# Context stores and input loads issued by GpSimd, and a count of 2.4 for the context's steps without weights

## The chip, the core and the metric

The kernel runs on one core of one Trainium2 chip. The core has five engines, each with its own instruction queue that is worked through in order: TensorE (PE, matrix products; PEld is its loading of weights), VectorE (DVE), ScalarE (ACT), GpSimd (POOL) and SyncE (SP, which here only issues transfers). Transfers between the device memory and the core's own memory (DMA) run on 16 DMA engines. The metric is the device time of one execution in microseconds (us).

## What is computed

Two transformer blocks run one after the other on 256 tokens of width 1024. The first block has a mixture of experts: 32 experts, four of them chosen for each token. The second block has two layers; it works on the latent tokens x and on a context of 256 further tokens. Cut to what matters:

```python
def moe_ffn(h, router_w, router_b, w_mlp1, b_mlp1, w_mlp2, b_mlp2):
    ...
    top_vals, top_idx = lax.top_k(logits, TOP_K)
    ...
    acc, _ = lax.scan(expert_step, acc0, (w_mlp1, b_mlp1, w_mlp2, b_mlp2, combine))

def second_block(x, c, ctx, c_ctx, ...):
    xc = ctx
    for l in range(DEPTH_2):
        ctx_out = l < DEPTH_2 - 1
        ...
        o, oc = token_mixers(modulate(x, sh1, sc1), modulate(xc, sh1c, sc1c), ...)
        x = layer_norm(DEEPNORM_ALPHA * x + g1 * (o @ w_out[l]), ...)
        x = layer_norm(DEEPNORM_ALPHA * x + g2 * swiglu(modulate(x, sh2, sc2), ...), ...)
        if ctx_out:
            xc = layer_norm(DEEPNORM_ALPHA * xc + g1c * (oc @ w_out[l]), ...)
            xc = layer_norm(DEEPNORM_ALPHA * xc + g2c * swiglu(modulate(xc, sh2c, sc2c), ...), ...)
    return x
```

The context xc does not depend on the first block. The latent tokens need from it, in each layer, only its keys and values and the final states of its linear attention.

## The kernel before

The program has three parts. In the first, the first block's attention runs and its router picks the experts. In the second, the 32 experts run, sorted by how many tokens they have: two of them with room for 128 tokens (rows), then sixteen with 64, then fourteen with 32. An expert's weights are twelve loads of 1 MB (`m_raw`), which SyncE issues into five buffers (`RAWS`); line 904 multiplies the first eight, line 962 the other four. Beside the experts the context of the second block runs. In the third part (`latent`) the latent tokens go through the second block's two layers.

The context is a generator (`context`, lines 1588 to 1667). Its steps yield a time, and `along` (line 1887) hands out credit: after each step of an expert the context gets 0.8, 1.45 or 3.2 (`SHARE`, for experts of 128, 64 and 32 rows) and advances until that is used up. Some steps work without weights: attention, the states of the linear attention (`gla_states`) and the linear attention itself (`gla`, with its decay steps in lines 1822 to 1826). These go through `dry`, which multiplies the time that they yield by `DRY`, so that they are spread further. After the last expert the rest of the context gets all the credit it wants.

This sets the order in which the code is written out. A scheduler then orders the instructions of each engine anew, by when it expects their inputs and the engine to be free. What runs is the order that it leaves on each engine.

The context's weights come by ScalarE's queue, in pieces of 512 KB (`w_raw`). Each is halved into two parts: ScalarE rounds it (`w_hi`, line 96) and GpSimd subtracts (`w_lo`, line 98). Each product is then three matmuls (lines 195 to 197). Four halved tiles fit. The products of the context go to the tile `c`, those of the latent part to `ps`.

The lines that the change touches: `keep` (line 1597) stores four tiles of keys and values (`nak`, `nav`, `gak`, `gav`) and later two states (`sf`, `sb`), once in each of two layers, so twelve stores; lines 1637 and 1642 load the context's input `x`, 1 MB, twice. The second load comes after the first layer's mixers, and `x` is scaled on GpSimd (line 1644, four instructions) before the output projection's sums are added to it. The small products of line 1543 (`ss`, on GpSimd, for a modulation) are placed in memory that other tiles have used before. The latent part reads the stored tiles back (line 1683), behind a branch (lines 1102 and 1103) that all engines pass after the last expert; more experts' work for overfull experts would stand behind it.

Of the kernel before, what the change touches and what calls it, by code (L numbers as in the profile page):

```python
# [37 lines left out]


SHARE = {128: 0.8, 64: 1.45, 32: 3.2}  # L40
DRY = 2.0
FILL = 0.8

FIRST = 2
# [87 lines left out]
class Build:  # L132
# [1455 lines left out]
    def context(self, w, ps, tag, saved):  # L1588


        nc, tc, io = self.nc, self.tc, self.io
        one = lambda n: tc.tile_pool(name=n, bufs=1, side="right")
        two = lambda n: tc.tile_pool(name=n, bufs=2, side="right")

        def keep(l, name, t):
            saved[l][name] = tc.dram_tile(list(t.shape), F32, name=f"kept_{name}_{l}")
            nc.sync.dma_start(saved[l][name], t)

        def halves(pu):
            return [pu.tile([P, KC, T], F32R, name=n) for n in ("uh", "ul")]  # L1600

        def mixers(l, u, pu, full):
            y = None
            with one("cg") as pg:
                o = {n: pg.tile(sh, F32, name=n) for n, sh in self.GLA_SHAPES + (self.FULL_SHAPES[2:] if full else ())}
                with one("cq") as pq:
                    o.update({n: pq.tile(sh, F32, name=n) for n, sh in self.SHAPES + (self.FULL_SHAPES[:2] if full else ())})
                    done = set()
                    with two("cp") as p2:
                        yield from self.projections(l, 1, u, o, w, p2, ps, tag, full, done)  # L1610
                    for n, _ in self.SHAPES:
                        keep(l, n, o[n])
                    if full:
                        y = halves(pu)
                        with two("ca") as p2:
                            yield from dry(self.attend(self.units(l, 1, o, None, done), *y, p2, ps, tag, done))
                with one("cl1") as p, two("cl2") as p2:
                    for n in ("sf", "sb"):
                        o[n] = p.tile([P, 64], F32, name=n)
                    yield from dry(self.gla_states(o, p2, ps, tag))  # L1620
                    for n in ("sf", "sb"):
                        keep(l, n, o[n])
                    if full:
                        yield from dry(self.gla(l, 1, o, None, *y, p, p2, ps, tag, done))
            return y

        def dry(steps):

            for c in steps:
                yield c and c * DRY  # L1630

        mod = [m[:, 1] for m in self.mod2]
        with one("cu") as pu:
            u = halves(pu)
            with one("cx") as px, two("ct") as p2:
                x = px.tile([P, KC, T], F32, name="x")
                nc.sync.dma_start(x, io["ctx"])
                yield from self.modulated(x, mod[0][:, 0:8], mod[0][:, 8:16], u, p2)
            y = yield from mixers(0, u, pu, True)
            with one("cx") as px:  # L1640
                x = px.tile([P, KC, T], F32, name="x")
                nc.sync.dma_start(x, io["ctx"])
                for k in range(0, KC, 2):
                    nc.gpsimd.tensor_scalar(x[:, k:k + 2], x[:, k:k + 2], ALPHA, None, op0=ALU.mult)
                for i in range(2):
                    with one("cf") as p:
                        acc = p.tile([P, KC, T], F32, name="acc")
                        if i == 0:
                            for ks in MIXED2:
                                yield from self.columns(acc, lambda k: (y[0][:, k], y[1][:, k]), ks, MIXED2[0][0], MIXED2[-1][1], w, ps, tag)  # L1650
                        else:
                            u = halves(pu)
                            with one("ch") as p1, two("ch2") as p2:
                                yield from self.modulated(x, *self.affine(mod[0], 1, 0, 0, p1), u, p2, None, normed)
                                self.settle(x, normed[0], 0, 0, p1)
                                yield from self.ffn(u, w, acc, p1, p2, ps, tag)
                        with two("cr2") as p2:
                            chunk, finish = self.norm(acc, mod[0][:, 24 * i + 16:24 * i + 24], x, px, p2, ps, tag)
                            for k in range(KC):
                                chunk(k)  # L1660
                                yield 0.4
                            normed = finish()
                            yield 1.8
                u = halves(pu)
                with two("ct") as p2:
                    yield from self.modulated(x, *self.affine(mod[1], 0, 0, 1, px), u, p2, None, normed)
                yield from mixers(1, u, pu, False)
# [410 lines left out]
```

## Time and profile before

| | us |
|---|---|
| median of 3 runs | 2369.41 |
| their range | 2366.2 to 2372.82 |
| profiled execution | 2358.65 |
| its span, first to last instruction | 2357.0 |

| engine | busy us | share of the span |
|---|---|---|
| TensorE matmuls | 2144.4 | 91% |
| TensorE loading weights | 1503.0 | 64% |
| VectorE | 1087.7 | 46% |
| ScalarE | 862.6 | 37% |
| GpSimd | 567.6 | 24% |

The execution moved 667.36 MB. The shares are means over parts with different limits, so that each part has to be read by itself. In the rows further down, a line of windows gives for each engine the busy time and, in brackets, the number of instructions; then the clock that TensorE was granted, as a share of full speed; the mean busy share of the 16 DMA engines; and what they moved. In a line of a timeline the brackets at the end tell how long the engine was idle before the instruction, and what ended the wait.

### The profile page before, as it was taken

Reading aid. Unit: us, or ns where it says so; the run is one execution under the profiler, and the core shown is the slowest. Engines: PE = TensorE matmul, PEld = TensorE weight load, DVE = VectorE, ACT = ScalarE, POOL = GpSimd, SP = SyncE. Lnnn points to the kernel's source line nnn. Section 1 sums busy time; section 2 is a strip of 40 time slices with the busy share of each in tenths; the row PEclk is TensorE's granted clock in tenths of the full one; section 3 lists DMA queues with packets and bytes.
Section 4 is the critical chain, followed back from the end, with each engine's and each line's share of the span. In section 5 each row is a group of like instructions: output and inputs, shape, how many; then the busy total and the mean of one; then the engine's idle time right before and its main releaser. Section 6 shows DMA issues by size and latency. Waiting matters only on the chain. (4 is left out here: it accounts for less than half of the span.)

```text
span 2357.0 us, 38285 instructions
## 1 busy us (share of the span) xinstructions
PE 2144.4 (91%) x15238; PEld 1503.0 (64%) x15239; DVE 1087.7 (46%) x2146; ACT 862.6 (37%) x1585; POOL 567.6 (24%) x335
## 2 busy tenths in 40 slices
PE   7899799999999988977999998968989999899998
PEld 4667533455444433524776765637879997788997
DVE  4765333221334322325443345227569767757434
ACT  2533201132232111213333333314555555466554
POOL 1001100122100000202444442504214443322442
PEclk8999799999999999977998999979999999999999
DMA  9867657899988899998999999993256754233553
GB/s 369 316 236 278 262 193 253 334 393 366 368 315 305 326 403 416 378 393 331 377 379 397 374 409 366 395 371 118 82 189 247 275 183 146 90 104 112 190 186 101
DMA packets 121721, 667.36 MB, mean 283 GB/s; under 512 B 14944, under 2 KB 16864, under 8 KB 62784
## 3 DMA queue, kind: packets, MB, share of 16 engines
q1 hardware_dynamic: 104016, 597.86, 67.5%
q10 hardware_dynamic: 17520, 66.99, 7.6%
q8 instruction: 122, 2.00, 0.3%
q14 instruction: 63, 0.52, 0.1%
HBM read 661.51 MB, written 3.28 MB: 282 GB/s over the span
## 5 line engine op out<-in xcount | busy, mean ns | idle before, releaser
L98 POOL TENSOR_TENSOR w_lo<-w_raw,w_hi 128x1024 fp32r<-128x1024 f32 x210 | 503.9, 2403 | 1098.8 <-ACT w_hi L96 890.1
L96 ACT ACTIVATE w_hi<-w_raw 128x1024 fp32r<-128x1024 f32 (+1 forms) x332 | 346.1, 1048 | 418.4 <-PE c L196 162.1
L904 PE MATMUL u<-m_raw,xT 128*64 128x512 f32 (+1 forms) x2048 | 396.0, 620 | 28.2 <-DMA m_raw<-in_w_mlp 28.2
L195 PE MATMUL ps<-uh,w_hi 128*128 128x256 f32 (+1 forms) x944 | 274.0, 291 | 10.4 <-ACT uh L1214 6.0
L197 PE MATMUL ps<-uh,w_lo 128*128 128x256 f32 (+1 forms) x944 | 270.5, 287 | 4.9 <-DVE w_lo L98 3.2
L196 PE MATMUL ps<-ul,w_hi 128*128 128x256 f32 (+1 forms) x944 | 270.7, 287 | 1.3 <-DVE ul L1215 1.2
L904 PEld LDWEIGHTS u<-m_raw,xT 128*64 128x64 f32 (+1 forms) x2048 | 103.8, 127 | 220.9 <-issue 172.5
L962 PE MATMUL y<-m_raw,aT 128*32 128x256 f32 (+1 forms) x1536 | 216.0, 507 | 19.1 <-DMA m_raw<-in_w_mlp 16.3
L98 DVE TENSOR_TENSOR w_lo<-w_raw,w_hi 128x1024 fp32r<-128x1024 f32 (+1 forms) x122 | 153.0, 1254 | 110.5 <-ACT w_hi L96 109.8
L195 PEld LDWEIGHTS ps<-uh,w_hi 128*128 128x128 f32 (+1 forms) x944 | 182.2, 193 | 17.7 <-ACT uh L1214 7.1
L197 PEld LDWEIGHTS ps<-uh,w_lo 128*128 128x128 f32 (+1 forms) x944 | 182.7, 194 | 5.9 <-DVE w_lo L98 3.9
L196 PEld LDWEIGHTS ps<-ul,w_hi 128*128 128x128 f32 (+1 forms) x944 | 183.0, 194 | 2.9 <-DVE ul L1215 2.0
L195 PE MATMUL c<-uh,w_hi 128*128 128x256 f32 (+1 forms) x584 | 172.0, 295 | 4.2 <-ACT uh L1214 3.1
L196 PE MATMUL c<-ul,w_hi 128*128 128x256 f32 (+1 forms) x584 | 170.7, 292 | 0.0
L197 PE MATMUL c<-uh,w_lo 128*128 128x256 f32 (+1 forms) x584 | 170.5, 293 | 0.0
L195 PE MATMUL ps<-hh,w_hi 128*128 128x256 f32 x560 | 163.8, 293 | 0.0
L197 PE MATMUL ps<-hh,w_lo 128*128 128x256 f32 x560 | 159.1, 284 | 1.2 <-DVE w_lo L98 1.2
L196 PE MATMUL ps<-hl,w_hi 128*128 128x256 f32 x560 | 159.4, 285 | 0.5 <-DVE hl L189 0.5
L962 PEld LDWEIGHTS y<-m_raw,aT 128*32 128x32 f32 (+1 forms) x1536 | 74.3, 129 | 131.8 <-issue 89.5
L914 DVE TENSOR_SCALAR glu<-u 128x512 f32<-128x512 f32 (+1 forms) x34 | 23.3, 687 | 236.4 <-PE u L904 236.3
L195 PEld LDWEIGHTS c<-uh,w_hi 128*128 128x128 f32 (+1 forms) x584 | 112.8, 193 | 25.1 <-issue 15.7
L196 PEld LDWEIGHTS c<-ul,w_hi 128*128 128x128 f32 (+1 forms) x584 | 113.2, 194 | 13.6 <-issue 10.9
(554 smaller groups left out, 3921.4 us busy)
## 6 DMA issues: line engine op xcount, KB each, us to landing
m_raw<-in_w_mlp SPq DMA_DIRECT2D x384, 1024.0 KB, 8.0
f_raw<-in_w_ada SPq DMA_DIRECT2D x47, 1024.0 KB, 7.1
w_raw<-in_w_ffn_in SPq DMA_DIRECT2D x88, 512.0 KB, 4.2
w_raw<-in_w_in SPq DMA_DIRECT2D x64, 512.0 KB, 5.0
w_raw<-in_w_ffn_in ACTq DMA_DIRECT2D x44, 512.0 KB, 8.6
w_raw<-in_w_ffn_out SPq DMA_DIRECT2D x44, 512.0 KB, 4.2
w_raw<-in_w_in ACTq DMA_DIRECT2D x34, 512.0 KB, 7.9
g_raw<-in_w_ada SPq DMA_DIRECT2D x16, 1024.0 KB, 8.4
```

Source lines behind the costliest of these rows:

```text
L96: nc.scalar.activation(hi, r, AF.Copy)
L98: e.tensor_tensor(lo, r, hi.bitcast(F32), op=ALU.subtract)
L195: nc.tensor.matmul(out, lh, rh, start=start, stop=False)
L196: nc.tensor.matmul(out, lh, rl, start=False, stop=False)
L197: nc.tensor.matmul(out, ll, rh, start=False, stop=stop)
L904: nc.tensor.matmul(u[z][r:r + s], xT[:, k, x0:x0 + s], ws[k - k0][:, c * 512:(c + 1) * 512], start=False, stop=k == KC - 2)
L914: nc.vector.tensor_scalar(glu, u0, 7.0, None, op0=ALU.min)
L962: nc.tensor.matmul(y[z][r:r + s], a[:, k], ws[(k - k0) // 2][:, k % 2 * D + c * wd:k % 2 * D + (c + 1) * wd], start=k == 3, stop=k == 4)
```

## The change

The twelve stores and the two input loads of the context are issued by GpSimd in place of SyncE, and `DRY` is 2.4 in place of 2.0:

```diff
-DRY = 2.0
+DRY = 2.4
...
         def keep(l, name, t):
             saved[l][name] = tc.dram_tile(list(t.shape), F32, name=f"kept_{name}_{l}")
-            nc.sync.dma_start(saved[l][name], t)
+            nc.gpsimd.dma_start(saved[l][name], t)
...
                 x = px.tile([P, KC, T], F32, name="x")
-                nc.sync.dma_start(x, io["ctx"])
+                nc.gpsimd.dma_start(x, io["ctx"])
                 yield from self.modulated(x, mod[0][:, 0:8], mod[0][:, 8:16], u, p2)
...
                 x = px.tile([P, KC, T], F32, name="x")
-                nc.sync.dma_start(x, io["ctx"])
+                nc.gpsimd.dma_start(x, io["ctx"])
```

The scheduler's order moves with it. On GpSimd, around the end of the first layer's linear attention, there stood before (the last decay step, the small products `ss`, eight halvings, the scaling of `x`):

```order
L1823 TENSOR_TENSOR gl_e<-gl_B 128x2x64
L1824 TENSOR_TENSOR gl_e<-gl_C 128x2x64
L1543 TENSOR_TENSOR ss<-vec_242,mod_1_266 128x8
L1545 TENSOR_TENSOR ss<-vec_242,mod_1_266 128x8
L1544 TENSOR_TENSOR ss<-ss,mod_1_266 128x8
L98 TENSOR_TENSOR w_lo<-w_raw,w_hi 128x1024 x8
L1644 TENSOR_SCALAR x<-x 128x512 x4
```

and now, on the same engine at the same place:

```order
L1823 TENSOR_TENSOR gl_e<-gl_B 128x2x64
L1824 TENSOR_TENSOR gl_e<-gl_C 128x2x64
L1642 DMA x<-in_ctx 128x2048
L1543 TENSOR_TENSOR ss<-vec_242,mod_1_266 128x8
L1545 TENSOR_TENSOR ss<-vec_242,mod_1_266 128x8
L1544 TENSOR_TENSOR ss<-ss,mod_1_266 128x8
L1644 TENSOR_SCALAR x<-x 128x512 x4
L98 TENSOR_TENSOR w_lo<-w_raw,w_hi 128x1024 x8
```

The input load stands right behind the last decay step, and the scaling of `x`, which needs it, now stands ahead of the eight halvings. The stores of the states (`kept_sf`, `kept_sb`) stand ahead of the first decay step on this queue.

On TensorE, after the first 24 matmuls of the context's output projection (lines 195 to 197), experts alone followed before, here from the last of these 24 on:

```order
L197 MATMUL c<-uh,w_lo 128x256
L904 MATMUL u<-m_raw,xT 64x512 x24
L894 MATMUL u<-b1h,bl 128x512
L962 MATMUL y<-m_raw,aT 64x512 x8
L929 MATMUL m<-ident,sg 128x128 x4
L894 MATMUL u<-b1h,bl 128x512
```

and now the context's matmuls stand between the experts' there:

```order
L197 MATMUL c<-uh,w_lo 128x256
L962 MATMUL y<-m_raw,aT 64x512 x8
L929 MATMUL m<-ident,sg 128x128 x4
L894 MATMUL u<-b1h,bl 128x512
L1012 MATMUL m<-selT,yh 128x256
L1012 MATMUL m<-selT,yl 128x256
L195 MATMUL c<-uh,w_hi 128x256
L196 MATMUL c<-ul,w_hi 128x256
```

The output projection thus goes on at once, where 208 matmuls of lines 904 and 962 stood between its first 24 matmuls and the rest.

At the end of the experts, TensorE's order was (line 1768 is the product that gives the second layer's states, line 1012 adds up an expert's outputs):

```order
L1012 MATMUL m<-selT,yl 128x256 x2
L962 MATMUL y<-m_raw,aT 32x256 x16
L1768 MATMUL c<-glv,gs_d 128x256 x3
L962 MATMUL y<-m_raw,aT 32x256 x16
L1768 MATMUL c<-glv,gs_d 128x256
L1012 MATMUL m<-selT,yh 128x256 x2
```

and is now:

```order
L1012 MATMUL m<-selT,yl 128x256 x2
L962 MATMUL y<-m_raw,aT 32x256 x32
L1012 MATMUL m<-selT,yh 128x256 x2
L1012 MATMUL m<-selT,yl 128x256 x2
L1012 MATMUL m<-selT,yh 128x256 x2
```

The states' products have moved ahead of the last six experts.

## Rows read from the trace of the kernel before

**Rows 1.** The span in 40 slices: TensorE, its clock, DMA, in tenths.
```profile
PE   7899799999999988977999998968989999899998
...
PEclk8999799999999999977998999979999999999999
DMA  9867657899988899998999999993256754233553
```

**Rows 2.** Windows, all engines: PE, PEld, DVE, ACT, POOL; clock, DMA share, GB/s.
```profile
450.00:660.00 210.00, 206.05 (x1178) 110.00 (x1180) 47.93 (x107) 60.81 (x122) 47.25 (x20) 1.00 0.97 372
840.00:930.00 90.00, 76.79 (x378) 29.12 (x380) 20.03 (x45) 11.80 (x19) 0.00 (x0) 0.98 0.99 405
832.00:1592.00 760.00, 663.99 (x4963) 415.24 (x4960) 273.81 (x520) 213.60 (x359) 216.51 (x100) 0.93 0.96 383
1140.00:1440.00 300.00, 281.54 (x2423) 214.10 (x2425) 119.74 (x208) 106.25 (x170) 134.52 (x56) 0.96 0.98 390
1530.00:1577.00 47.00, 31.73 (x276) 13.55 (x268) 11.23 (x22) 5.49 (x10) 0.42 (x1) 0.78 0.98 404
1595.00:2357.00 762.00, 715.02 (x5936) 662.32 (x5936) 483.71 (x843) 415.35 (x755) 261.39 (x150) 0.98 0.47 156
...
1080.00:1140.00 60.00, 52.41 (x412) 37.91 (x412) 32.64 (x66) 25.20 (x49) 19.91 (x13) 0.89 0.86 334
1860.00:1920.00 60.00, 60.00 (x505) 60.00 (x504) 38.15 (x43) 32.51 (x49) 24.75 (x12) 1.00 0.64 206
```

**Rows 3.** Windows, TensorE's matmuls of line 904 alone.
```profile
450.00:660.00 210.00, 80.88 (x356) 1.00 0.97 372
840.00:930.00 90.00, 43.00 (x184) 0.98 0.99 405
1140.00:1440.00 300.00, 52.84 (x443) 0.96 0.98 390
```

**Rows 4.** Windows, TensorE's matmuls of line 962 alone.
```profile
450.00:660.00 210.00, 36.54 (x160) 1.00 0.97 372
840.00:930.00 90.00, 21.92 (x96) 0.98 0.99 405
1140.00:1440.00 300.00, 28.72 (x448) 0.96 0.98 390
```

**Rows 5.** Windows, TensorE's matmuls on the context's tile c alone.
```profile
450.00:660.00 210.00, 77.43 (x536) 1.00 0.97 372
...
1140.00:1440.00 300.00, 183.92 (x1362) 0.96 0.98 390
```

**Rows 6.** Timeline of GpSimd, 777 to 1070 us: start, duration, instruction, wait before.
```profile
777.16 0.48 POOL L1824 TENSOR_TENSOR gl_e<-gl_C 128x128 f32<-128x128 f32 x1
941.12 0.20 POOL L1543 TENSOR_TENSOR ss<-vec,mod 128x8 f32<-128x8 f32 x1 [163.48 <-DMA kept_sb<-sb]
...
945.55 2.35 POOL L98 TENSOR_TENSOR w_lo<-w_raw,w_hi 128x1024 fp32r<-128x1024 f32 x1 [3.90 <-ACT w_hi L96]
...
1064.17 5.88 POOL L1644 TENSOR_SCALAR x<-x 128x512 f32<-128x512 f32 x4 [47.29 <-DMA x<-in_ctx]
```

**Rows 7.** Timeline of SyncE: one store and the second input load.
```profile
932.90 0.43 SPq L1597 DMA_DIRECT2D kept_sb<-sb  x1
...
1052.29 0.36 SPq L1642 DMA_DIRECT2D x<-in_ctx  x1
```

**Rows 8.** Timeline of all engines at the end of the experts.
```profile
1570.41 0.43 SPq L1597 DMA_DIRECT2D kept_gav<-gav  x1
...
1575.24 1.93 PE L962 MATMUL y<-m_raw,aT 128*32 128x256 f32 x32 [0.16 <-DMA m_raw<-in_w_mlp]
1580.56 0.60 ACT L1756 ACTIVATE gs_d<-c 128x512 f32<-128x512 f32 x1 [6.44 <-DMA kept_gav<-gav]
...
1581.54 2.93 PE L1768 MATMUL c<-glv,gs_d 128*128 128x256 f32 x6 [4.37 <-DVE gs_d L1763]
...
1584.39 3.01 PE L962 MATMUL y<-m_raw,aT 128*32 128x256 f32 x32
```

## Prediction

> **What bounds the kernel now.** I read the 40 slices first [rows 1]. Two of the stretches there matter. In slices 8 to 27, about 412 to 1591 us, the DMA digit is 8 or 9: the experts' weights stream in, and the second block's context is woven between the experts. From slice 28 on the DMA digit is 2 to 7 while TensorE stands mostly at 9: the latent part, bound by TensorE. The change touches the first of these two. I then cut it into windows [rows 2]. Over 832 to 1592 us the DMA share is 0.96 at 383 GB/s, and TensorE is busy 664 of 760 us. So DMA is the limit, with TensorE close behind it, and which of the two ends last depends on which experts the context stands beside. Three windows give the prices:
>
> - 840 to 930 us: experts of 64 rows with no context. Such an expert leaves 64 records of line 904 and 32 of line 962. 184 and 96 records [rows 3, 4] are 2.92 experts, 30.9 us each. DMA is at 0.99; TensorE is busy 76.8/2.92 = 26.3 us per expert.
> - 450 to 660 us: the same experts with context. 356 and 160 records are 5.38 experts, 39.1 us each, with 536/5.38 = 99.7 context matmuls each [rows 3 to 5]. TensorE is busy 206 of 210 us, DMA at 0.97: TensorE is the limit. One context matmul costs it 60/505 = 0.119 us (the saturated window of rows 2), and 26.3 + 99.7 x 0.119 = 38.2 us agrees with 206/5.38 = 38.3.
> - 1140 to 1440 us: experts of 32 rows (64 records of each line) with context. 443 and 448 records are 6.96 experts, 43.1 us each, with 195.7 context matmuls each. DMA is at 0.98 [rows 2 to 5]. Without context such an expert needs its twelve loads of 1024 KB, 12.58 MB, at the 404 GB/s of 1530 to 1577 us [rows 2]: 31.1 us. So a context matmul, with its share of the weights, costs (43.1 - 31.1)/195.7 = 0.061 us there.
>
> A context matmul is thus about half as dear beside a 32-row expert, where DMA is the limit, as beside a 64-row one, where TensorE is.
>
> **Where the context stands now.** GpSimd's last decay step ends at 777 us. Its next instruction, a small product of line 1543, starts at 941 us after 163.5 us of waiting for the store of sb [rows 6]. That store is issued by SyncE at 932.9 us, since it stands in SyncE's queue behind the experts' loads [rows 7]. The eight halvings of weights (line 98) stand behind line 1543, so TensorE has no context to work on and runs experts alone. The context's input is then loaded at 1052 us [rows 7], and GpSimd waits 47.3 us for it [rows 6]. So the context is held back, and ends only with the experts: the states' products (line 1768) wait for the store of gav, and the last expert's product waits behind them, from 1577.2 (1575.24 + 1.93) to 1584.4 us [rows 8].
>
> **The change, part by part.**
> *The count of 2.4.* With the count put back to 2.0 and the queue change kept, the order of instructions is the same on every engine, apart from numbers in names. It costs nothing here.
> *The stores and loads on GpSimd.* The order of the latent part is the same on all engines, so the 762 us from 1595 us on [rows 2] stay. In the stage before, the context moves forward. I count it against the experts' own matmuls (lines 904 and 962: 1856 up to the branch; the 64-row experts, 48 each, stand at 192 to 960, the 32-row ones, 64 each, from 960 on). Context matmuls done, before and now: at 640, 974 and 950; at 960, 1142 and 1656; all 3043 are done at 1856 and at 1472. So the terms are:
>
> 1. *64-row experts, 640 to 960* (6.67 of them). Before: 168 context matmuls, 25 each: 30.9 + 25 x 0.061 = 32.4 us. Now 706, 106 each: TensorE is the limit, 39.1 + 6 x 0.119 = 39.8 us. 7.4 x 6.67 = **+49.3 us**. Were it bound by DMA, 30.9 + 106 x 0.061 = 37.4 us, it would be +33; I take the first, since 450 to 660 us is the same mixture, with TensorE at 98%.
> 2. *32-row experts* (14). Before: 1901 context matmuls, 136 each: 31.1 + 136 x 0.061 = 39.4 us, 552 us in all. Now 1387 lie beside the first eight, 173 each: 41.7 us, 334 us; the last six run alone, 31.1 us each, 187 us. **-31.5 us**.
> 3. *Before 640*: 24 context matmuls fewer, at 0.061 to 0.119 us: **-2 us**.
> 4. *The end*: the last expert's product no longer stands behind the states' products: **-7.2 us** (1584.4 - 1577.2), at least -4 if its own data landed late.
> 5. *The norm of the context at 1080 to 1140 us*: DMA falls to 0.86, with the clock at 0.89 after a stretch beside 32-row experts alone [rows 2]; against 0.98 that is 60 x 0.12 = 7 us. Now it stands beside 64-row experts, where the clock is 0.98 to 1.00. I take half of it: **-3.5 us** (0 to -7).
> 6. *GpSimd's own queue*: it issues 14 DMAs more. SyncE takes 0.36 to 0.43 us for one [rows 7, 8]; GpSimd's price is in no row. Even at the 2.4 us that it takes for a halving (2.35 us, rows 6) that is 34 us, in a stage where it is busy 217 of 760 us [rows 2]: hidden, **0**, unless TensorE comes to wait for it. Its most exposed place is the second input load: behind it stand four scalings (5.9 us, rows 6) and then the halvings. Before, that load took 1064.2 - 1052.3 = 11.9 us to land [rows 6, 7], so 17.8 us in all. What covers it: four halved tiles are ready, and in TensorE's new order 56 expert matmuls (0.457 us each: 43.00/184 x 2 records) and 96 context ones stand before the first that needs a fifth, 25.6 + 11.4 = 37 us. Even with the 2.4 us of the halving, some 17 us are spare. The store of sf now waits on GpSimd for the four stores ahead of it, and what is queued behind are the decay steps, which need the states' step anyway: 0, at worst one landing, some 10 us (kept_gav: issued at 1570.4, its waiter starts at 1580.6, rows 8).
>
> Sum: 49.3 - 31.5 - 2 - 7.2 - 3.5 + 0 = **+5 us**. SyncE's queue, freed of 14 issues, gains nothing that I count, because its loads wait for free buffers.
>
> The profiled execution took 2358.65 us (span 2357.0), 10.8 us below the median of 2369.41. The sum is made against it, giving 2364; against the median, **2374 us**. A measurement of this kernel tells about 0.3%, 7 us, from no change, so this is "the same", on the slow side.
>
> **The rivals.**
> *Faster: nothing in the mixture waits for TensorE.* If the 64-row experts with context are held by DMA alone, term 1 is +33, and with the whole of terms 4 and 5 the sum is 33 - 31.5 - 2 - 7.2 - 7 = -15 us: 2355 us. For it: the bytes are the same in both kernels and the DMA share is 0.96 over the stage, so nothing but lost DMA time can be lost or won. Against: TensorE at 206 of 210 us in the window with that mixture.
> *Slower: GpSimd's queue comes last.* The input load lands late, the halvings stand behind it, and TensorE, which runs in order, stands at the first context matmul without weights while the experts' loads fill their five buffers. It decides from a landing of about 12 + 17 = 29 us on. If each of the two input loads took the 47 us that GpSimd once waited for one [rows 6], the second costs 47 - 29 = 18 us; with terms 1 to 5 (+5) that is +23 us: 2392 us. Against: an input load took 12 us, and the first one stands where VectorE and TensorE have other work.
> The Trainium skill ("SBUF — State Buffer", section "SBUF: two separate sides") warns against just this move: VectorE in some of its modes locks GpSimd out of a shared port, so that a DMA issued by GpSimd stands without descriptors. No run here shows it yet; by its rule the waiting would go with VectorE's work.
> VectorE is busy 274 of 760 us in the stage [rows 2], 36%, in instructions of 0.53 us (274/520), so a start would be put off by single instructions, not by tens of us; this gives the rival little.
> *Also slower: the six experts at the end run at the low clock.* In 1530 to 1577 us the clock was 0.78, with TensorE busy 31.7 of 47 us and DMA at 0.98 [rows 2], so DMA still set the pace. Should TensorE come to need 33 us for one instead of 31.1, that is 6 x 2 = 12 us: +17, 2386 us.
> *The change does not do what it says*: the order shows the new places, and that the count of 2.4 moves nothing. What is left is that the forward move has no effect at all, 2369 us, inside the forecast.
>
> **How the numbers follow.** Chances: forecast (within 7 us of the median before, including no effect) 0.40; GpSimd's queue or the low clock or a dearer mixture, beyond +7 us, 0.35; DMA alone as the limit, below -7 us, 0.25. The forecast's own range is 2362 to 2381. The range for 8 in 10 runs from the faster rival, 2355, to the slower one, 2392: outside lie mainly a further gain from smoother DMA and both slow rivals at once.
>
> **What would show it.** Right: line 1543 on GpSimd no longer waits some 160 us; context matmuls run on where GpSimd stood still from 777 to 941 us; between it and the last 64-row expert TensorE is at 97% or more and DMA at 0.95 to 0.97, with about 40 us per expert; the last 185 us before the latent part show experts alone at 400 GB/s with the clock below 0.9; no wait of the last product for line 1768; latent part 762 us. Wrong: long idle times of line 98 behind the input load or the stores on GpSimd; a DMA share below 0.93 in the 64-row mixture; or the experts at the end at more than 33 us each.

## The result

The changed kernel takes 2383.93 us (median of 8 runs), the kernel before 2365.29 us (8 runs beside it): a ratio of 1.008, 95% interval 1.0051 to 1.0108, that is **18.6 us slower** (12 to 26). My 2374 us was too low by 10 us; the range of 2355 to 2392 held the time. "The same" was the likeliest of my three cases with 0.40, and it was the wrong one: the loss is beyond 0.3%, where I had put 0.35, and of the three causes named there it is the dearer mixture.

The profiled execution of the changed kernel took 2385.84 us, with a span of 2384.2 us. Its slices, to set against [rows 1] (TensorE, its clock and DMA, 40 slices of 59.6 us):

```profile
PE   6899799999999999999998896768998999899998
...
PEclk8988799999999999999999898788999999999999
DMA  9866756899988888999999998994247754233553
```

TensorE is at 9 from slice 6 to 21; before, it had 8s in slices 15 and 16 and 7s in 18 and 19, where the clock fell too. DMA now stays at 8 up to slice 16, before only up to 14. In slices 25 to 27 TensorE is at 6 and 7 with a clock of 7 to 8: experts alone.

From here on I cut the traces at the same work, not at the same time: at the counts of the experts' matmuls that the prediction uses (192, where the 64-row experts begin, 640, 960 and the end). Windows of all engines, with the columns of [rows 2], of the changed kernel:

```profile
426.60:800.90 374.30, 360.96 (x2007) 184.08 (x2003) 113.43 (x273) 99.74 (x210) 58.76 (x41) 0.99 0.92 349
800.90:1079.90 279.00, 266.99 (x1548) 151.89 (x1549) 104.25 (x206) 78.07 (x134) 65.57 (x37) 0.98 0.91 346
1079.90:1612.90 533.00, 440.78 (x3620) 277.26 (x3620) 177.14 (x335) 142.61 (x241) 154.98 (x70) 0.91 0.97 389
```

and of the kernel before, the same work:

```profile
419.20:793.00 373.80, 361.20 (x2035) 185.36 (x2031) 118.01 (x284) 101.07 (x213) 55.92 (x35) 1.00 0.92 349
793.00:1015.40 222.40, 198.99 (x1078) 91.27 (x1077) 55.90 (x118) 38.20 (x59) 17.91 (x11) 0.99 0.96 386
1015.40:1587.00 571.60, 497.61 (x4054) 338.10 (x4058) 222.94 (x406) 181.96 (x312) 198.60 (x90) 0.90 0.96 381
```

The first stretch (192 to 640) is the same. The second (640 to 960) costs 279.0 - 222.4 = **+56.6 us**, the third 533.0 - 571.6 = **-38.6 us**, and what lies behind it 771.3 against 770.0 us. That makes some +20 us. The first stretch also starts 7.4 us later than before, but so it does without the change: in the profiles below it starts anywhere from 419 to 432 us, so this is chance of one execution, and the difference of the two spans (27 us) is larger than that of the medians for it.

What TensorE waited for from 801 to 1080 us in the changed kernel (engine, line, releaser: us in all, times, longest):

```profile
PE m L929 <- DVE sg L921: 3.7, 2, 2.0
PE m L863 <- DVE rows L850: 2.5, 2, 1.7
PE u L894 <- DVE sg L920: 2.1, 2, 1.7
PE u L894 <- DVE glu L914: 0.9, 1, 0.9
PE c L1803 <- DVE gl_A L1829: 0.8, 2, 0.5
PE c L1494 <- DVE nm_z L1502: 0.8, 1, 0.8
```

and for the same work before, 793 to 1015 us:

```profile
PE u L904 <- DMA m_raw<-in_w_mlp: 13.5, 8, 2.8
PE y L962 <- DMA m_raw<-in_w_mlp: 3.2, 3, 1.7
```

This is the change in four words: the limit has moved. Before, TensorE waited 16.7 us for the experts' weights. Now no such wait stands among the rows; the weights wait for TensorE, and DMA falls from 0.96 to 0.91. Of the 12.0 us in which TensorE is still idle (279.0 - 266.99), 10.8 are waits for VectorE.

GpSimd's timeline (start, duration, instruction, wait before), against [rows 6]:

```profile
820.36 0.56 POOL L1642 DMA_DIRECT2D x<-in_ctx  x1 [20.84 <-PE c L1873]
820.94 0.22 POOL L1543 TENSOR_TENSOR ss<-vec,mod 128x8 f32<-128x8 f32 x1
...
827.45 5.89 POOL L1644 TENSOR_SCALAR x<-x 128x512 f32<-128x512 f32 x4 [6.00 <-DMA x<-in_ctx]
838.61 4.90 POOL L98 TENSOR_TENSOR w_lo<-w_raw,w_hi 128x1024 fp32r<-128x1024 f32 x2 [5.27 <-PE c L197]
```

The wait of 163.5 us is gone, the load lands within 7.1 us of its issue, and the halvings begin 5.3 us after the scaling.

### The profile page after: what moved, and what is told of

Read it like the earlier page. It is cut to its first block, busy times and chain, and to the rows that moved or that the text cites. A ratio compares the mean times of both kernels' runs of the same rounds, so it can differ in the third digit from the quotient of the medians.

```text
span 2384.2 us, 38329 instructions
## 1 busy us (share of the span) xinstructions
PE 2160.0 (91%) x15238; PEld 1506.4 (63%) x15239; DVE 1087.8 (46%) x2146; ACT 862.0 (36%) x1585; POOL 572.4 (24%) x349
## 5 line engine op out<-in xcount | busy, mean ns | idle before, releaser
L904 PE MATMUL u<-m_raw,xT 128*64 128x512 f32 (+1 forms) x2048 | 405.3, 641 | 35.3 <-DMA m_raw<-in_w_mlp 35.3
L962 PE MATMUL y<-m_raw,aT 128*32 128x256 f32 (+1 forms) x1536 | 221.5, 519 | 21.3 <-DMA m_raw<-in_w_mlp 15.5
L914 DVE TENSOR_SCALAR glu<-u 128x512 f32<-128x512 f32 (+1 forms) x34 | 23.4, 687 | 222.5 <-PE u L904 222.4
L197 PEld LDWEIGHTS c<-uh,w_lo 128*128 128x128 f32 (+1 forms) x584 | 109.9, 188 | 18.2 <-issue 14.6
```

Source lines behind the costliest of these rows:

```text
L197: nc.tensor.matmul(out, ll, rh, start=False, stop=stop)
L904: nc.tensor.matmul(u[z][r:r + s], xT[:, k, x0:x0 + s], ws[k - k0][:, c * 512:(c + 1) * 512], start=False, stop=k == KC - 2)
L914: nc.vector.tensor_scalar(glu, u0, 7.0, None, op0=ALU.min)
L962: nc.tensor.matmul(y[z][r:r + s], a[:, k], ws[(k - k0) // 2][:, k % 2 * D + c * wd:k % 2 * D + (c + 1) * wd], start=k == 3, stop=k == 4)
```

## The experiments

Times between milestones in us, read off the records of lines 904 and 962 in each profile (a record is one entry of the trace; a matmul of these two lines leaves two), beside the timed ratio to the kernel before. The ratio comes from 5 to 12 runs of each changed kernel, the times from one execution. "Alone" with stores and loads means with the count of 2.4, as in the whole change:

| Kernel | Ratio (95%) | 192 to 640 | 640 to 960 | 960 to end | Sum |
|---|---|---|---|---|---|
| before | 1 | 373.8 | 222.4 | 571.6 | 1167.8 |
| after | 1.0080 (1.0051 to 1.0108) | 374.3 | 279.0 | 533.0 | 1186.3 |
| issued by ScalarE | 1.0061 (1.0041 to 1.0082) | 374.6 | 282.4 | 529.7 | 1186.7 |
| moved, count 2.0 | 1.0084 (1.0054 to 1.0114) | 374.0 | 280.7 | 536.5 | 1191.2 |
| stores alone, count 2.4 | 0.9993 (0.9978 to 1.0008) | 374.7 | 237.8 | 563.7 | 1176.2 |
| loads alone, count 2.4 | 1.0000 (0.9981 to 1.0019) | 373.7 | 215.0 | 579.2 | 1167.9 |
| count 2.2 alone | 0.9977 (0.9954 to 1.0000) | 378.4 | 219.4 | 573.0 | 1170.8 |
| count 2.4 alone | 0.9924 (0.9899 to 0.9950) | 378.4 | 215.0 | 558.8 | 1152.2 |
| the same again | 0.9942 (0.9920 to 0.9964) | 377.1 | 218.2 | 563.6 | 1158.9 |
| count 2.6 alone | 0.9988 (0.9967 to 1.0010) | 378.3 | 209.4 | 580.9 | 1168.6 |
| count 2.8 alone | 1.0087 (1.0062 to 1.0112) | 378.3 | 211.9 | 584.2 | 1174.4 |
| shares 0.7 and 4.5 | 1.0020 (0.9999 to 1.0042) | 353.3 | 226.3 | 595.4 | 1175.0 |
| shares 0.5 and 5 | 1.0033 (1.0012 to 1.0053) | 352.4 | 203.8 | 619.4 | 1175.6 |
| shares 0.4 and 7 | 1.0234 (1.0201 to 1.0266) | 352.7 | 202.7 | 666.3 | 1221.7 |

The theory I tested I call "place": what counts is beside which experts the context's matmuls stand. Its rival, "queue": GpSimd issuing DMAs costs something itself.

### Who issues: ScalarE in place of GpSimd

```
-            nc.gpsimd.dma_start(saved[l][name], t)
+            nc.scalar.dma_start(saved[l][name], t)
-                nc.gpsimd.dma_start(x, io["ctx"])        (both loads)
+                nc.scalar.dma_start(x, io["ctx"])
```

> The changed kernel with the context's 12 stores and 2 input loads issued by ScalarE in place of GpSimd; TensorE's order, with the context matmuls done by each expert, is that of the changed kernel (950 at 640, 1656 at 960, all 3043 at 1472). Theory 'place': the change costs what it costs because the context now stands beside 64-row experts, whoever issues the DMAs: +19 us against the kernel before as the changed kernel has it, 1.006 to 1.010, with 640 to 960 at some 279 us (222 before) and 960 to the end at some 533 (572 before). Theory 'queue': what exceeds my +5 comes from GpSimd issuing DMAs: without it +5 us or less, below 1.004.

Measured 1.0061, +15.7 us by the medians (2383.26 and 2367.53). The two stretches after 640, in the columns of [rows 2]:

```profile
801.10:1083.50 282.40, 270.42 (x1544) 152.78 (x1543) 104.25 (x206) 77.86 (x134) 64.97 (x36) 0.97 0.90 342
1083.50:1613.20 529.70, 440.41 (x3622) 277.58 (x3620) 177.30 (x335) 142.59 (x241) 151.54 (x64) 0.91 0.97 392
```

They are those of the changed kernel within 4 us, and so is their sum: 192 to the end takes 1186.7 against 1186.3 us. The intervals of the two ratios overlap. GpSimd as the issuer costs nothing that can be seen. The issues themselves (bytes and median us from issue to landing), of after:

```profile
x<-in_ctx POOLq DMA_DIRECT2D x2, 1024.0 KB, 6.2
kept_nav<-nav POOLq DMA_DIRECT2D x2, 384.0 KB, 6.5
```

of before

```profile
x<-in_ctx SPq DMA_DIRECT2D x2, 1024.0 KB, 8.3
kept_nav<-nav SPq DMA_DIRECT2D x2, 384.0 KB, 9.6
```

and with ScalarE:

```profile
x<-in_ctx ACTq DMA_DIRECT2D x2, 1024.0 KB, 6.0
kept_nav<-nav ACTq DMA_DIRECT2D x2, 384.0 KB, 9.0
```

GpSimd's land as early as any. The Trainium skill ("SBUF — State Buffer", section "SBUF: two separate sides") says that a DMA issued by GpSimd can stand while VectorE holds the port that the two share; the runs here give no sign of it, with VectorE busy 104 of 279 us in the stretch.

### One half of the change at a time

The stores alone, with the count of 2.4 (against the kernel before):

```
-DRY = 2.0
+DRY = 2.4
-            nc.sync.dma_start(saved[l][name], t)
+            nc.gpsimd.dma_start(saved[l][name], t)
```

> One part of the change alone: the stores are issued by GpSimd, the two input loads by SyncE as before (count 2.4). The context then stands still at 1142 matmuls from 740 to about 1100, held by the second input load, and is done by 1790, one expert before the end. Theory 'place': 640 to 960 takes what it took before (192 context matmuls against 168: some 224 us against 222), 960 to the end about 7 us less since the last product no longer stands behind the states' products: -6 us in all, 0.995 to 1.000. Theory 'queue': 12 of the 14 DMAs are still on GpSimd, so most of the +19 stays: 1.005 or more.

The loads alone, with the count of 2.4 (against the kernel before):

```
-DRY = 2.0
+DRY = 2.4
-                nc.sync.dma_start(x, io["ctx"])          (both loads)
+                nc.gpsimd.dma_start(x, io["ctx"])
```

> The other part alone: the two input loads are issued by GpSimd, the stores by SyncE as before (count 2.4). The context stands still at 974 matmuls from 640 to about 930, held by the stores, and is done by 1664, three experts before the end. Theory 'place': 640 to 960 as before (170 context matmuls against 168), 960 to the end 7 us less: -7 us, 0.994 to 1.000; the last three experts run alone at some 31 us each. Theory 'queue': the late input load is the part of it that reaches TensorE, so the loss stays here: 1.005 or more.

Measured 0.9993 and 1.0000, where both together give 1.0080. Against the kernel before neither half seems to cost anything, but both contain the count of 2.4, which alone is a gain (0.9924 and 0.9942, next section). What a half costs is read against that kernel: in the same set of runs the medians are 2365.07 (stores) and 2367.79 us (loads) against 2353.17 us (count alone), 12 and 15 us slower. The gain of the count hides both.

The stretch from 640 to 960, with the stores alone and then with the loads alone:

```profile
794.20:1032.00 237.80, 207.07 (x1104) 97.10 (x1103) 61.66 (x131) 39.65 (x62) 19.99 (x11) 0.97 0.93 363
```

```profile
802.90:1017.90 215.00, 189.00 (x999) 80.82 (x998) 49.03 (x111) 34.25 (x55) 13.13 (x11) 0.98 0.98 396
```

TensorE keeps 31 and 26 us of slack there, against 12 with the whole change. Tile c has 261 and 156 records there, against 701; with the count alone it has 156. SyncE's queue held the context back at two points one behind the other, the stores of sf and sb and then the second input load. Each half of the change takes one hold away and leaves the other; GpSimd waits 203.06 us for the load with the stores alone:

```profile
1107.12 5.88 POOL L1644 TENSOR_SCALAR x<-x 128x512 f32<-128x512 f32 x4 [203.06 <-DMA x<-in_ctx]
```

Only without both does the context run through beside the 64-row experts. Where the halves lose against the count alone, by single executions: the stores from 640 to 960 (237.8 us against 215.0 and 218.2) and at the end, where TensorE stands for the states' products (between 1540 and 1596 us), for which it never waits in the two runs of the count alone:

```profile
PE c L1768 <- DVE gs_d L1763: 7.8, 1, 7.8
```

The loads lose behind 960 (579.2 us against 558.8 and 563.6), not beside 64-row experts. So the halves do not decide against the "queue" rival, since with 12 of the 14 DMAs on GpSimd 12 of some 35 us are lost; it falls by the run with ScalarE alone. The 6 to 7 us that I had expected of both from the end, against the kernel before, did not come in full: -2.5 us (-5 to +2) and 0 (-4 to +4), although the count, which I had priced at nothing, was in them.

### The count alone, and the move alone

The count alone is

```
-DRY = 2.0
+DRY = 2.4
```

> The count of 2.4 alone, all DMAs of the context on SyncE as before. The context falls behind by 30 to 60 expert matmuls from 1088 on (1143 done at 1088 against 1274, 2216 at 1472 against 2425), none of it moved from 32-row to 64-row experts. Theory 'place': no change, 0.998 to 1.002 (0 +- 5 us), since 32-row experts take the same matmuls at the same price. Rival 'count': the count is what costs: 1.005 or more.

Measured **0.9924**, 14 us faster by the medians (12 to 24 by the interval), where I had expected nothing. The move with the count left at 2.0:

> The change without its count: stores and loads on GpSimd, steps without weights at 2.0 as before. Its order is that of the changed kernel on every engine. Theory 'place': what the changed kernel has, 1.006 to 1.010 against the kernel before, 192 to the end of the experts in some 1186 us (before 1168): once the context's DMAs stand outside SyncE's queue, the count has nothing to move. Rival 'count': the count alone took 14 us off in the experiment on it, so without it the moved DMAs come out some 14 us worse than the change: 1.012 or more.

Measured 1.0084, as with the count. With the DMAs outside SyncE's queue the count has nothing to move; with them in it, it is worth 14 us. So against the count alone, the move of the DMAs costs some 35 us (1.008 against 0.992 and 0.994): 640 to 960 takes 279.0 us in place of 215.0, 960 to the end 533.0 in place of 558.8. What the count does is to let the two holds end later: the second input load is issued at 1094.8 us in place of 1052.3 [rows 7].

To see whether this was chance, the series of counts, all else as before:

> The count at 2.2, all DMAs on SyncE. The second half of the context stands half as far back as with 2.4 (1174 at 1088 against 1274 at 2.0 and 1143 at 2.4; 2319 at 1472 against 2425 and 2216), done at 1792. Theory 'end and norm': the 14 us that 2.4 took off are the wait of the last product at the end (5 to 7 us) and the lost DMA time around the norm (some 7 us); the first goes as soon as the context is done ahead of the last expert, the second by how far the norm is moved: -5 to -14 us, 0.994 to 0.998. Rival 'luck of place': which block of context matmuls meets which expert decides, so neighbours differ by 10 us either way: 0.998 or more is as likely.

> The count at 2.4 alone a second time, on another chip or day. Both theories: -14 +- 5 us again, 0.991 to 0.996, with 192 to the end of the experts in some 1152 us. Were the first time chance of the machine, 0.997 or more.

> The count at 2.6. 1040 at 960 (1142 with 2.4), 2109 at 1472, 3000 at 1792, done at some 1830, ahead of the last expert's product by little. Theory 'end and norm': as 2.4 or up to 5 us worse at the end, 0.992 to 0.997. Rival 'luck of place': 0.998 or more as likely.

> The count at 2.8. 996 at 960, 2031 at 1472, 2914 at 1792, done only with the last expert (3039 at 1856, 3043 behind it). Theory 'end and norm': the wait at the end is back (5 to 7 us) and the last context matmuls outlast the experts, the norm's part of the gain stays: 0.995 to 0.999. Rival 'later is always better': 0.990 or less.

Measured 0.9977, 0.9942, 0.9988 and 1.0087: by these ratios -5, -14, -3 and +20 us. The gain of 2.4 came twice and is clear of noise; those of 2.2 and 2.6 are not, their intervals reaching to 1.0000 and 1.0010. Of the five counts, 2.4 is the best, with both sides falling off. Its place, by work (960 to 1152, 1152 to 1792, 1792 to the end), first before:

```profile
1015.40:1150.00 134.60, 106.60 (x760) 61.13 (x760) 53.47 (x106) 39.26 (x75) 32.02 (x20) 0.82 0.92 366
1150.00:1369.20 219.20, 205.42 (x1737) 156.21 (x1736) 84.63 (x155) 78.89 (x128) 96.61 (x41) 0.95 0.98 382
1369.20:1565.50 196.30, 170.55 (x1420) 113.22 (x1420) 80.53 (x134) 61.74 (x108) 69.97 (x30) 0.94 0.97 393
1565.50:1587.00 21.50, 15.04 (x138) 7.54 (x142) 4.31 (x12) 2.05 (x4) 0.00 (x0) 0.68 0.88 356
```

and with the count of 2.4 (first run of it):

```profile
1025.30:1145.60 120.30, 90.07 (x649) 44.33 (x648) 48.49 (x97) 27.06 (x50) 22.18 (x17) 0.86 0.97 395
1145.60:1567.70 422.10, 394.95 (x3348) 292.39 (x3347) 172.94 (x303) 155.45 (x262) 187.74 (x79) 0.96 0.98 389
1567.70:1584.10 16.40, 11.20 (x132) 5.35 (x136) 2.96 (x5) 2.17 (x5) 0.17 (x1) 0.79 1.01 417
```

The stretch with the context's norm takes 14 us less: it has 181 records of tile c in place of 294, and DMA is at 0.97 in place of 0.92. With 77 more that have left the stretch ahead of it, some 190 records come to the next one, and cost 6.6 us there (422.1 against 219.2 + 196.3 = 415.5). The end takes 5 us less, the products of the states now running behind the last expert's product (from 1588.5 us on). The second run has 120.7, 424.8 and 18.1 us there. These are my terms 5 and 4, which I had credited to the change; the count earns them, and the change does not keep the first.

How DMA comes to be lost in that stretch shows in 4 us of the kernel before:

```profile
1111.00:1115.00 4.00, 4.00 (x17) 3.55 (x18) 0.65 (x2) 0.16 (x1) 0.00 (x0) 0.50 1.01 421
1115.00:1119.00 4.00, 4.00 (x24) 3.46 (x27) 0.00 (x0) 1.06 (x1) 0.70 (x1) 0.50 0.08 29
```

Just before, TensorE has stood twice for VectorE:

```profile
1106.77 0.47 PE L894 MATMUL u<-b1h,bl 128*128 128x512 f32 x1 [2.27 <-DVE sg L920]
1109.44 0.69 PE L929 MATMUL m<-ident,sg 64*128 64x64 f32 x4 [2.21 <-DVE sg L921]
```

Now, at the lower of its two clocks (0.50, 1.2 GHz), it works through context matmuls that stand ahead of the expert's product (line 962, at 1118.3 us) in its queue, and DMA stops (0.08, 29 GB/s). SyncE's next loads wait for that line, for 14.6 us at the longest between 1059 and 1126 us:

```profile
SPq L113 <- PE y L962: 26.9, 8, 14.6
```

With 2.8 the context ends after the experts. From the last expert matmul on, TensorE still has these of the tile c:

```profile
1598.80:1609.60 10.80, 7.86 (x60) 7.25 (x61) 0.00 (x0) 0.79 (x3) 1.00 0.29 102
```

and the latent part's first load of a saved tile is issued 22 us behind the experts (1598.8), where before it came 8.7 us behind them (1595.69 - 1587.0):

```profile
1620.83 0.34 SPq L1683 DMA_DIRECT2D c_nak<-kept_nak  x1
```

Why 2.2 and 2.6 give so little, with the context only some 80 to 110 records off, I have not settled. The profiles show where it is lost: 1472 to 1792 takes 217.0 and 221.9 us in place of 209.3 and 208.2 with 2.4, at a granted clock of 0.90 and 0.93 in place of 0.96 and 0.97. "Luck of place" cannot be ruled out for the middle of the series; for 2.8 the rows above show 13 of the 20 us.

### Still later: the shares

Here the context is pushed further towards the 32-row experts, all DMAs on SyncE:

```
-SHARE = {128: 0.8, 64: 1.45, 32: 3.2}
+SHARE = {128: 0.8, 64: 0.7, 32: 4.5}     DRY = 2.4
+SHARE = {128: 0.8, 64: 0.5, 32: 5}       DRY = 2.4
+SHARE = {128: 0.1, 64: 0.4, 32: 7}       DRY = 2.0
```

> All DMAs on SyncE, the count 2.4, and the shares of the context 0.7 for 64-row steps and 4.5 for 32-row steps in place of 1.45 and 3.2. The context is 853 at 640 (974 with the count alone), 974 at 960 (1142), and is done with the experts at 1856: 289 context matmuls more beside 32-row experts, at most 245 for one expert there. Theory 'place': 121 of them go from 0.082 us ((39.1 - 30.9)/99.7) to 0.061 us, the 168 others cost the same in both, so -2 us against the kernel with the count alone: 2351 us, 0.990 to 0.996 against before. Rival 'later is always better': another 10 us off, below 0.989.

> As the run before, with shares of 0.5 and 5: 853 at 640 and still at 900, 861 at 960, and done at 1792; the densest 32-row experts have 274 context matmuls. By my prices a 32-row expert is bound by TensorE from some 240 on (17 + 0.119 n against 31.1 + 0.061 n us), so four experts lose some 2 us each: about +5 us against the run before, 0.992 to 0.998. Rival 'later is always better': another 5 us off, below the run before.

> All DMAs on SyncE, count 2.0, shares of 0.1, 0.4 and 7 for steps of 128, 64 and 32 rows. The context stands at 853 until 960 and then runs at 316 matmuls per 32-row expert, done at 1536, with five experts alone behind. Theory 'place' with TensorE as the limit from 240 on: six such experts take 17 + 316 x 0.119 = 54.6 us each where DMA alone would need 31.1 + 316 x 0.061 = 50.4, so +25 us, and against the kernel with the count alone +20 to +35: 2375 to 2388 us, 1.003 to 1.009. Rival 'only DMA counts in the 32-row stage': no more than +5 against the kernel with the count alone, 0.990 to 0.996.

Measured 1.0020, 1.0033 and 1.0234: 2368, 2372 and 2416 us, all worse than I said, by 17, 10 or more, and 28 us or more. Both rivals fall too: later is not always better, and TensorE does count in the 32-row stage. No run moved the context earlier with its DMAs left on SyncE. What was wrong were my prices, and these runs show how. Five 32-row experts (1472 to 1792, or 1152 to 1472 in the last row), with the records on the tile c from the same windows of that tile alone:

| Five experts of | c records per expert | us per expert | us per record more than in the row above |
|---|---|---|---|
| after, 1442.1 to 1595.7 | 1 | 30.7 | |
| count 2.4, 1358.4 to 1567.7 | 174 | 41.9 | 0.065 |
| shares 0.7 and 4.5, 1342.8 to 1578.4 | 230 | 47.1 | 0.093 |
| shares 0.4 and 7, 1127.9 to 1434.5 | 322 | 61.3 | 0.154 |

The row for the last, in the columns of [rows 2], and then of tile c alone (TensorE first):

```profile
1127.90:1434.50 306.60, 291.51 (x2371) 226.90 (x2374) 144.95 (x254) 129.21 (x220) 161.84 (x73) 0.97 0.85 317
```

```profile
1127.90:1434.50 306.60, 212.86 (x1612) 196.77 (x1612) 59.10 (x118) 3.14 (x6) 0.97 0.85 317
```

The price of a matmul is 0.065 us while DMA is the limit and 0.15 us when TensorE is (291.5 of 306.6 us busy, DMA at 0.85). The row between is not clear of scatter: in the changed kernel five experts with the same 174 records each (1216.7 to 1442.1 us) took 45.1 us each, not 41.9, which makes the price there 0.083 us. In the 64-row stage it is the same the other way round. From 192 to 640, with 154 records of tile c fewer, the stretch is 25 us shorter, first with the count of 2.4 and then with the shares:

```profile
431.90:810.30 378.40, 365.81 (x2033) 187.10 (x2029) 117.95 (x284) 101.12 (x213) 55.97 (x35) 0.98 0.90 345
```

```profile
428.90:782.20 353.30, 339.03 (x1879) 168.92 (x1875) 91.35 (x211) 90.33 (x193) 49.59 (x21) 1.00 0.93 362
```

That is 0.163 us each, twice the 0.082 us that I had taken as (39.1 - 30.9)/99.7. The gain of 25 us is lost again, 11 us from 640 to 960 and 37 behind 960, where the same matmuls stand beside the experts that are left (595.4 against 558.8 us).

**The best kernel** of all is the one before with the count of 2.4 and nothing else: 0.9924 and 0.9942 in two sets of runs.

## Why the prediction was half right

1. *64-row experts, 640 to 960*: +49.3 said, +56.6 measured. The mechanism is the one I named, TensorE as the limit, and its work was right: 267.0/6.67 = 40.0 us busy per expert, where I had 39.8 for the whole. What I left out is the 12.0 us in which TensorE is idle there, 10.8 of them waiting for VectorE (the wait rows above). While DMA is the limit such waits can hide behind it; once TensorE is, each of them is added. **This is the step that failed**: I took the price of an expert from the window at 450 to 660 us, with TensorE at 98%, and in its 5.38 experts TensorE waits for VectorE only this long:

```profile
PE m L863 <- DVE rows L850: 0.8, 1, 0.8
```

The norm of the context, which that window does not have, explains some of the difference: between 885 and 936 us, where the norm stands, are 4.2 of the 10.8 us. What else VectorE was doing stands in the last section. The stage before was dearer than I said, too: 222.4/6.67 = 33.3 us in place of 32.4. My price is per record, and the 168 context matmuls there leave 233 records, 35 for each expert in place of 25; with these it comes to 33.0 us.

2. *32-row experts* and 4. *the end*: -31.5 - 7.2 = -38.7 said, -38.6 measured. Part of this agreement is luck. The eight experts with context took 362.2/8 = 45.3 us, not 41.7 (they carry 185 records of tile c each, 1483 in 362.2 us), while the last six took 170.8 us (153.6 + 17.2), not 187; the stage before took 571.6 us in place of 552 + 7.2. Some 12 us too little on both sides fell out of the difference. At the end the last product no longer waits for line 1768, as said. But the wait has moved and not gone: line 1768 now runs at 1441 to 1449 us, beside the eight experts, and TensorE stands ahead of it:

```profile
1440.97 1.22 PE L1768 MATMUL c<-glv,gs_d 128*128 128x256 f32 x2 [7.98 <-DVE gs_d L1763]
```

DMA falls with it, to 0.80 from 1433 to 1441 us and 0.51 from 1441 to 1449, which is some 5 us of transfers. My sum has no term for it; it is part of what the eight experts took too much.

3. *Before 640*: -2 said, +0.5 measured.
5. *The norm of the context*: -3.5 said; nothing of it is to be seen. It now stands beside 64-row experts, where the clock is up as I said, but where TensorE is the limit, so that its waits (4.2 us) are part of the 12 us of point 1. I had moved a cost out of one stage without asking what it costs in the other.
6. *GpSimd's queue*: 0 said, and nothing that shows was measured, by the run with ScalarE. The issue of the second input load takes 0.56 us, and the load 7.1 us to land, far from the 29 us at which the rival would have decided.

The sum is 56.6 - 38.6 + 0.5 = +18.5 us, where I had +5: 7.3 us of the difference are in term 1, 3.5 in term 5, 2.5 in term 3. The measured median is only 10 us above my 2374, not 13.5, since the median of three runs that I started from lay 4 us above that of the eight: that part is luck.

The rival "nothing in the mixture waits for TensorE" fell with the wait rows. "Low clock at the end" fell as well: the clock was 0.79 there, and an expert took 30.7 us. Of the signs that I named, the wait of line 1543, the tail's 30.7 us and the latent part came as said; TensorE came to 96%, not 97, and an expert to 41.8 us, not 40; a DMA share of 0.91 in the 64-row mixture, which I had named as a sign against me, came too, and it said rightly that the term was too small.

*The count* costs nothing within the change, as said. But I asked only what it does beside the other edit. Alone it is the one good half.

## What to carry over

Moving a DMA off an in-order queue can take away a brake that was doing good: before you free a stage, ask which work it will then run beside, and price it by what is the limit there. A price worked out as an average over a mixture holds only at its own density; the next matmul more costs little while transfers are the limit and somewhat more than its own time when the engine is (0.154 us against 212.86/1612 = 0.132 in the row of tile c above). Where a change has two edits, cost each of them alone too, and read every part against the kernel that differs from it by that part only: here the gain of the count hid the cost of each half.

## What I had not expected of the hardware

Most of TensorE's waits for VectorE in the changed kernel's 64-row stage stand behind VectorE instructions that took far longer than usual, each while a halving (line 98) ran on GpSimd. The first of them, the same line without a halving beside it, and the wait that followed:

```profile
841.35 2.70 DVE L919 TENSOR_TENSOR glu<-glu,sg 128x512 f32<-128x512 f32 x1 [0.40 <-ACT sg L918]
930.04 0.68 DVE L919 TENSOR_TENSOR glu<-glu,sg 128x512 f32<-128x512 f32 x1
845.56 0.66 PE L929 MATMUL m<-ident,sg 128*128 128x128 f32 x4 [1.75 <-DVE sg L921]
```

The halving beside it is in GpSimd's timeline above (838.61 to 843.51 us). From 800.9 to 1079.9 us there are ten such VectorE instructions, 16.5 us longer in all than the same ones without GpSimd at work, and 9.1 of the 10.8 us of waits end within 6 us after one of them; the profiles with ScalarE as the issuer and with the count of 2.0 show the same ten. Line 1479, which adds a matmul's result, takes 0.69 us beside GpSimd as well. In the kernel before there are two in this stage, 1.9 us in all. So the context beside the 64-row experts brings with it not only matmuls but halvings, beside which the experts' VectorE work is slower. That this makes the waits is read off their order in time; no run was made to test what the change would cost without it.

Three kernels with one order of TensorE's instructions and different issuers or counts agree within 5 us from the first 64-row expert to the last expert (1186.3, 1186.7, 1191.2), and two executions of the kernel with the count of 2.4 within 7 (1152.2, 1158.9). What a single profile shows below that says nothing about a change.
